# Six columns of zero rows a batch instead of seven, with one shared column for the few rows beyond them

**Chip, cores, metric.** One core of one Trainium2 chip. The time is that of the device for one execution, in microseconds (us).

## The reference

```python
# scores (8, 2048, 2048) f32, values (8, 2048, 2560) f32
best_j = np.argmax(scores, axis=2)
gathered = values[b_idx, best_j, :].copy()
out = np.zeros_like(values)
np.add.at(out, (b_idx, best_j, slice(None)), gathered)
```

An output row is thus the value row with the same number, times how many score rows picked it: about 750 rows of a batch are picked once, 550 more often, and 750 never.

## The kernel before

VectorE counts for every row how often it was picked, and builds lists of row numbers. GpSimd then issues indirect transfers of 128 entries each: copies of once-picked rows straight from `values` to `out`, gathers of the oftener picked (ScalarE scales them, then they are scattered), and scatters of a row of zeros to the rows never picked. An entry that names no row holds a number past the end and is skipped.

```python
ZCAP, MCAP = 7, 5          # zero columns and gather columns of a batch, 128 entries each
ZLAST = 12                 # zero columns of the last batch
FETCH = {2: 5, 3: 12}      # rows of other traffic booked for DMA engines 2 and 3
...
# value_steps(b): after the counts
first = (NT, NT // 2, 4)[min(b, 2)]        # row copies issued ahead of the gathers
for t in range(first):
    copy_once(t)
...
def zeros(columns):
    for k in columns:
        scatter(zrow[:], zi[:, k:k + 1], free_running)
        if rest:
            copy_once(rest.pop(0))
...
nz = ZLAST if b == B - 1 else ZCAP
if b == 0: ...
else:
    gathers()                              # five, with a row copy after each
    zeros(range(ZHEAD))                    # four
for k in range(MCAP):
    scatter(staged[k], mi[:, k:k + 1], ...)
if b > 0:
    zeros(range(ZHEAD, nz))
```

In the last batch a routine on VectorE (`level_engines`) adds up how many rows each of the 16 DMA engines has to move, and deals that batch's zero rows so that the engines come out equal.

## Time and profile before

| | value | how to read it |
|---|---|---|
| time, median of the first three runs | 824.42 us (824.17 to 825.19) | the spread is larger than the effect that is looked for |
| 4-byte packets of the GpSimd queue | 17,974 | skipped entries and completion marks |
| zero-row transfers | 61 | 7 x 7 + 12 |
| rows moved | 20,762 | the work itself, not touched by the change |

The lines of the page and of the stages stand in the prediction.

### The profile page before, as it was taken

The numbers are of one execution on the slowest core, as the hardware profiler recorded it, in microseconds if no ns is written. First come the engines' busy times: TensorE is split into PE (matmuls) and PEld (weight loads), VectorE is DVE, ScalarE is ACT, GpSimd is POOL, SyncE is SP. The second block draws the span as 40 slices with busy tenths as digits, with TensorE's granted clock in tenths as the row PEclk, the third lists the DMA queues.
The fourth block names the chain that finished last, engine by engine and source line by source line (L and its number), as shares of the span: only waits on it lengthen the run. The fifth ranks groups of instructions, "written<-read, shape, count | busy, mean of one in ns | idle before, by whom it ended". The sixth has DMA issues, their size and how long they took to land.

```text
span 824.0 us, 2978 instructions
## 1 busy us (share of the span) xinstructions
PE 31.8 (4%) x786; PEld 29.1 (4%) x786; DVE 600.3 (73%) x737; ACT 168.1 (20%) x107; POOL 271.3 (33%) x277
## 2 busy tenths in 40 slices
PE   0211210000000000000000000000000000000000
PEld 0111110000000000000000000000000000000000
DVE  5887779999999999999999999999998000000000
ACT  6664730041012100023000032000320230230140
POOL 0027241011233504201513200615166356346442
DMA  9999999999999999999999999999999999999997
GB/s 385 426 437 429 433 412 410 441 419 425 427 423 427 428 427 435 429 428 420 429 427 421 429 428 430 433 428 412 426 425 424 423 427 422 424 424 422 425 425 288
DMA packets 44949, 347.12 MB, mean 421 GB/s; under 512 B 18662, under 2 KB 18662, under 8 KB 18662
## 3 DMA queue, kind: packets, MB, share of 16 engines
q0 software_dynamic: 38736, 212.67, 62.1%
q1 hardware_dynamic: 6192, 134.22, 38.0%
q8 instruction: 6, 0.10, 0.0%
q14 instruction: 15, 0.12, 0.0%
HBM read 354.42 MB, written 300.15 MB: 794 GB/s over the span
## 4 chain that ended last, share of the span: by engine, by line
DMA 35%; DVE 27%; another core or an unknown queue 23%; ACT 5%; POOL 5%; issue 4%; PE 0%; SPq 0%; ACTq 0%; POOLq 0%; DVEq 0%
DMA room<-in_values_dram,many_i 23%; DVE am L201 9%; DVE mx L200 9%; DMA out_dram<-room,many_i 8%; DVE mx L224 5%; ACT room L417 4%; DMA room<-in_scores_dram 4%; POOL out_dram L33 3%; ACT less L227 2%; POOL out_dram L182 2%; POOL room L177 1%; DVE oh L378 1%; DVE oh_lo L210 1%; DVE sole L234 0%
## 5 line engine op out<-in xcount | busy, mean ns | idle before, releaser
L201 DVE FIND_INDEX8 am<-mx,room 128x8 uint32<-128x2048 f32 x96 | 219.3, 2285 | 0.0
L200 DVE MAX8 mx<-room 128x8 f32<-128x2048 f32 x96 | 218.7, 2278 | 0.0
L417 ACT ACTIVATE room<-room,many_c 128x2560 f32<-128x2560 f32 x40 | 96.6, 2426 | 587.6 <-DMA room<-in_values_dram,many_i 587.6
L33 POOL DMA_INDIRECT out_dram<-in_values_dram,ones_i x128 | 130.3, 1018 | 106.3 <-DVE m L349 67.9
L182 POOL DMA_INDIRECT out_dram<-room,many_i x40 | 38.7, 966 | 258.0 <-ACT room L417 254.9
L177 POOL DMA_INDIRECT room<-in_values_dram,many_i x40 | 41.2, 1029 | 155.2 <-DMA out_dram<-room,many_i 137.0
L224 DVE MAX8 mx<-room 128x8 f32<-128x2048 f32 x32 | 72.8, 2286 | 11.4 <-DMA room<-in_scores_dram 11.4
L227 ACT ACTIVATE less<-room,mx 128x2048 bf16<-128x2048 f32 x32 | 64.0, 2001 | 38.4 <-DVE sole L234 17.4
L182 POOL DMA_INDIRECT out_dram<-zrow,zero_i x61 | 60.1, 985 | 18.6 <-issue 18.3
L218 PE MATMUL cnt_ps<-oh_hi,oh_lo 128*128 128x16 bf16 x96 | 6.1, 174 | 418.0 <-DVE oh_hi L214 418.0
L218 PEld LDWEIGHTS <-oh_lo 128*128 128x128 bf16 x96 | 6.3, 104 | 417.9 <-DVE oh_lo L210 397.9
L237 PEld LDWEIGHTS <-less 128*128 128x128 bf16 x512 | 16.1, 104 | 83.3 <-ACT less L227 59.6
L378 DVE TENSOR_TENSOR oh<-lo,fill_f 128x2048 f16<-128x2048 uint32 x8 | 18.3, 2291 | 0.3
L237 PE MATMUL cnt_ps<-sole,less 128*128 128x1 bf16 x512 | 18.1, 165 | 0.0
L210 DVE TENSOR_TENSOR oh_lo<-lo,lane_f 128x512 bf16<-128x512 uint32 x24 | 16.6, 693 | 0.4
L234 DVE TENSOR_SCALAR sole<-n_less 128x1 bf16<-128x1 f32 x32 | 4.8, 149 | 14.9 <-ACT less L227 14.7
L201 DVE MATCH_VALUE_LOAD am<-mx,room 128x8 f32 x96 | 8.8, 92 | 3.3
L235 PE MATMUL cnt_ps<-sole,minus 128*128 128x16 bf16 x32 | 5.5, 172 | 82.9 <-DVE sole L234 81.1
L396 PE MATMUL l_ps<-put,oh 128*128 128x32 f16 x128 | 4.7, 188 | 70.9 <-DVE put L393 70.9
L396 PEld LDWEIGHTS <-oh 128*128 128x128 f16 x128 | 4.6, 104 | 72.0 <-DVE oh L378 61.6
L227 ACT ACTIVATION_READ_ACCUMULATOR less<-room,mx 128x1 f32 x32 | 6.0, 186 | 0.0
L206 DVE TENSOR_SCALAR lo<-am 128x4 uint32<-128x4 uint32 x24 | 5.3, 222 | 0.8
(104 smaller groups left out, 80.7 us busy)
## 6 DMA issues: line engine op xcount, KB each, us to landing
room<-in_scores_dram SPq DMA_DIRECT2D x24, 4096.0 KB, 17.5
room<-in_scores_dram SPq DMA_DIRECT2D x9, 2048.0 KB, 13.1
room<-in_scores_dram SPq DMA_DIRECT2D x8, 1024.0 KB, 5.8
room<-in_scores_dram SPq DMA_DIRECT2D x2, 3072.0 KB, 13.9
out_dram<-in_values_dram,ones_i POOLq DMA_INDIRECT x128
out_dram<-zrow,zero_i POOLq DMA_INDIRECT x61
room<-in_values_dram,many_i POOLq DMA_INDIRECT x40, 45.0
out_dram<-room,many_i POOLq DMA_INDIRECT x40, 46.5
```

What stands on the lines that cost most here:

```text
L33: return eng.add_instruction(ins)
L177: note(nc.gpsimd.indirect_dma_start(out=v, out_offset=None, in_=values_flat[:, :], in_offset=bass.IndirectOffsetOnAxis(ap=idx, axis=0), bo ...
L182: note(nc.gpsimd.indirect_dma_start(out=out_flat[:, :], out_offset=bass.IndirectOffsetOnAxis(ap=idx, axis=0), in_=v, in_offset=None, bound ...
L200: nc.vector.max(out=mx[:], in_=rows)
L201: nc.vector.max_index(out=am[:, g, :], in_max=mx[:], in_values=rows)
L210: nc.vector.tensor_tensor(out=oh_lo[:], in0=lo[:].unsqueeze(2).to_broadcast([P, G, P]), in1=lane_f[:].unsqueeze(1).to_broadcast([P, G, P]) ...
L218: nc.tensor.matmul(out=cnt_ps[:], lhsT=oh_lo[:, k, :], rhs=oh_hi[:, k, :], start=(t == G - 1 and k == 0), stop=(t == NT - 1 and k == G - 1))
L224: nc.vector.max(out=mx[:], in_=rows)
L227: nc.scalar.activation(out=less[:], in_=rows, func=mybir.ActivationFunctionType.Sign, bias=mx[:, 0:1], scale=-1.0, accum_out=n_less[:])
L237: nc.tensor.matmul(out=cnt_ps[:, c:c + 1], lhsT=less[:, c * P:(c + 1) * P], rhs=w, start=False, stop=(t == NT - 1 and c == NT - 1))
L378: nc.vector.tensor_tensor(out=oh[:], in0=lo[:].unsqueeze(2).to_broadcast([P, NT, P]), in1=fill_f[:].unsqueeze(1).to_broadcast([P, NT, P]), ...
L417: nc.scalar.activation(out=v, in_=v, func=mybir.ActivationFunctionType.Copy, bias=0.0, scale=mc[:, k:k + 1])
```

## The change

Its intent: batches 0 to 6 have 748 to 780 rows of zeros. Six columns hold 768, so the seventh is nearly empty. It is dropped, and the rows beyond 768 of all seven batches go to one column at the very end. VectorE has to work out each such row's place in it.

```diff
-    ZCAP, MCAP = 7, 5
+    ZCAP, MCAP = 6, 5
+    left_n, left_f, unfit: three small tiles, filled at the start        (abridged)
 # level_engines
+        nc.vector.tensor_scalar(out=left_e[:], in0=up_f[:], scalar1=left_n[:, 0:1], scalar2=None, op0=ALU.add)
+        (two more: the shared column's rows join the engines' loads)
-        first = (NT, NT // 2, 4)[min(b, 2)]
+        first = (NT, NT // 2, 5)[min(b, 2)]
 # value_steps, b < B - 1, after the ranks
+            nc.vector.tensor_scalar(out=n_b[:], in0=tots[:, 0, b:b + 1], scalar1=-float(ZCAP * P), scalar2=0.0, op0=ALU.add, op1=ALU.max)
+            (ten more: does the batch's rest fit, move its ranks behind those of earlier batches)
 # value_steps, after the lists
+            (three more: take the batch's entries over into left_f)
 # value_steps, at its end
         if b > 0:
             zeros(range(ZHEAD, nz))
+        if b == B - 1:
+            scatter(zrow[:], left_i[:, 0:1], free_running)
```

More of the change, by code (lines that the diff above doesn't have):

```diff
@@ L118 @@
     tots = consts.tile([P, 2, B], FP32)
+    left_n = consts.tile([P, 1], FP32)
+    nc.vector.memset(left_n[:], 0.0)
+    left_f = consts.tile([P, 1], FP32)
+    nc.vector.memset(left_f[:], BIG)
+    unfit = consts.tile([P, 1], FP32)
+    nc.vector.memset(unfit[:], 0.0)
     most = consts.tile([P, 1], FP32)
@@ L151 @@
     ones_i = ctx.enter_context(nc.sbuf_tensor([P, B * NT], INT32))
+    left_i = ctx.enter_context(nc.sbuf_tensor([P, 1], INT32))
     zero_i = ctx.enter_context(nc.sbuf_tensor([P, B * NT], INT32))
@@ L281, in level_engines @@
         nc.vector.tensor_reduce(out=load[:, 1, :], in_=share[:, :, B:2 * B], op=ALU.add, axis=X)
+        left_e = lev.tile([P, NE], INT32)
+        nc.vector.tensor_scalar(out=left_e[:], in0=up_f[:], scalar1=left_n[:, 0:1], scalar2=None, op0=ALU.add)
+        nc.vector.tensor_single_scalar(out=left_e[:], in_=left_e[:], scalar=4, op=ALU.logical_shift_right)
+        nc.vector.tensor_tensor(out=load[:, 0, :], in0=load[:, 0, :], in1=left_e[:], op=ALU.add)
         work = lev.tile([P, NE], FP32)
@@ L368, in value_steps @@
             nc.vector.tensor_scalar(out=rank[:, c, :], in0=base[:, c, :], scalar1=off_ps[:, c:c + 1], scalar2=None, op0=ALU.add)
+        unfit_b = fin.tile([P, 1], FP32)
         if b == B - 1:
             level_engines(rank[:, 0, :])
+        else:
+            n_b = fin.tile([P, 1], FP32)
+            nc.vector.tensor_scalar(out=n_b[:], in0=tots[:, 0, b:b + 1], scalar1=-float(ZCAP * P), scalar2=0.0, op0=ALU.add, op1=ALU.max)
+            fit_b = fin.tile([P, 1], FP32)
+            nc.vector.tensor_tensor(out=fit_b[:], in0=n_b[:], in1=left_n[:], op=ALU.add)
+            nc.vector.tensor_scalar(out=unfit_b[:], in0=fit_b[:], scalar1=float(P), scalar2=BIG, op0=ALU.is_gt, op1=ALU.mult)
+            nc.vector.tensor_tensor(out=unfit[:], in0=unfit[:], in1=unfit_b[:], op=ALU.max)
+            nc.vector.tensor_single_scalar(out=fit_b[:], in_=fit_b[:], scalar=float(P), op=ALU.is_le)
+            shift_b = fin.tile([P, 1], FP32)
+            nc.vector.tensor_tensor(out=shift_b[:], in0=left_n[:], in1=fit_b[:], op=ALU.mult)
+            past = fin.tile([P, NT], FP32)
+            nc.vector.tensor_scalar(out=past[:], in0=rank[:, 0, :], scalar1=float(ZCAP * P), scalar2=shift_b[:, 0:1], op0=ALU.is_ge, op1=ALU.mult)
+            nc.vector.tensor_tensor(out=rank[:, 0, :], in0=rank[:, 0, :], in1=past[:], op=ALU.add)
+            nc.vector.tensor_tensor(out=n_b[:], in0=n_b[:], in1=fit_b[:], op=ALU.mult)
+            nc.vector.tensor_tensor(out=left_n[:], in0=left_n[:], in1=n_b[:], op=ALU.add)
+            nc.vector.tensor_tensor(out=tots[:, 0, b:b + 1], in0=tots[:, 0, b:b + 1], in1=n_b[:], op=ALU.subtract)
         hi = fin.tile([P, 2, NT], U32)
@@ L409, in value_steps @@
         nc.vector.tensor_copy(mc, l_ps[:, NM:2 * NM])
+        if b < B - 1:
+            x = 2 * NM + ZCAP
+            left_b = fin.tile([P, 1], FP32)
+            nc.vector.scalar_tensor_tensor(out=left_b[:], in0=e[:, x:x + 1], scalar=float(b * S - 1), in1=l_ps[:, x:x + 1],
+                                           op0=ALU.add, op1=ALU.add)
+            nc.vector.tensor_tensor(out=left_b[:], in0=left_b[:], in1=unfit_b[:], op=ALU.add)
+            nc.vector.tensor_tensor(out=left_f[:], in0=left_f[:], in1=left_b[:], op=ALU.min)
+        else:
+            nc.vector.tensor_copy(left_i[:], left_f[:])
         rest = list(range(first, NT))
@@ L472 @@
             pass
-        full = fin.tile([1, 2], FP32)
-        nc.vector.tensor_reduce(out=full[:, 0:1], in_=tots[0:1, 0, 0:B - 1], op=ALU.max, axis=mybir.AxisListType.X)
-        nc.vector.tensor_reduce(out=full[:, 1:2], in_=tots[0:1, 1, :], op=ALU.max, axis=mybir.AxisListType.X)
+        full = fin.tile([1, 1], FP32)
+        nc.vector.tensor_reduce(out=full[:], in_=tots[0:1, 1, :], op=ALU.max, axis=mybir.AxisListType.X)
         worst = fin.tile([P, 1], BF16)
@@ L481 @@
         nc.vector.tensor_single_scalar(out=over[:, 3:4], in_=sole_ps[0:1, :], scalar=-float(P), op=ALU.is_gt)
-        nc.vector.tensor_single_scalar(out=over[:, 0:1], in_=full[:, 0:1], scalar=float(ZCAP * P), op=ALU.is_gt)
-        nc.vector.tensor_single_scalar(out=over[:, 1:2], in_=full[:, 1:2], scalar=float(MCAP * P), op=ALU.is_gt)
+        nc.vector.tensor_single_scalar(out=over[:, 0:1], in_=unfit[0:1, :], scalar=0.0, op=ALU.is_gt)
+        nc.vector.tensor_single_scalar(out=over[:, 1:2], in_=full[:], scalar=float(MCAP * P), op=ALU.is_gt)
         nc.vector.tensor_single_scalar(out=over[:, 2:3], in_=most[0:1, :], scalar=float(ZLAST * LE), op=ALU.is_gt)
```

## The prediction

> **What bounds the kernel now.** I began with the page: busy shares, the 40 slices, the DMA queues. VectorE looks like the fullest engine (73%), but the slices say when.
>
> ```profile
> DVE  5887779999999999999999999999998000000000
> ...
> DMA  9999999999999999999999999999999999999997
> GB/s 385 426 437 429 433 412 410 441 419 425 427 423 427 428 427 435 429 428 420 429 427 421 429 428 430 433 428 412 426 425 424 423 427 422 424 424 422 425 425 288
> ...
> q0 software_dynamic: 38736, 212.67, 62.1%
> q1 hardware_dynamic: 6192, 134.22, 38.0%
> ```
>
> VectorE is full until slice 31 (640 us) and then has nothing to do; the DMA engines are full from the first slice to the last. The two queues' packet times add up to 100.1% of 16 engines' span. The same in stages, with each engine's busy time, clock, DMA share and GB/s at the end of a line:
>
> ```profile
> 550.00:640.00 90.00, 2.74 (x52) 2.40 (x52) 86.27 (x137) 12.03 (x5) 42.31 (x42) 1.00 1.01 423
> 640.00:720.00 80.00, 0.00 (x0) 0.00 (x0) 0.07 (x1) 16.87 (x7) 37.27 (x38) 1.00 1.02 425
> 760.00:800.00 40.00, 0.00 (x0) 0.00 (x0) 0.00 (x0) 12.14 (x5) 17.56 (x18) 1.00 1.02 424
> 800.00:824.00 24.00, 0.00 (x0) 0.00 (x0) 0.00 (x0) 0.00 (x0) 7.74 (x8) 1.00 0.75 306
> ```
>
> The rate is the same while VectorE works (423) and when it has finished (425), and the DMA share is 1.01 to 1.02 throughout. So the kernel ends when its DMA engines have moved their packets. The chain of waits names VectorE and GpSimd for parts of the span, but in none of them did the DMA engines run dry. From the packet records in the trace I counted, moment by moment, how many packets were in flight: between the first load and the last 15 us, missing engines add up to 0.11 us of the span; in the last 8 us, in which engines finish one after another, to 3.6 us. At the start it is the 2.8 us before the first load.
>
> So the question is what one packet costs. The records sort by size. There are 20,762 packets of 10,240 B (a row of values or of output), 386 ns each on average, 501.4 us of the span when divided over 16 engines; the score loads are 313.2 us. Then queue 0 has 17,974 packets of 4 B, recorded at 9 ns each, 10.1 us over 16 engines. Of those, 269 indirect transfers x 16 = 4,304 are completion marks. The 269 transfers have 269 x 128 = 34,432 index entries; less the 20,762 rows that leaves 13,670: the entries whose index is out of range. A skipped entry thus still costs a 4-byte packet, but a tiny one.
>
> **What the Trainium skill says.** "DMA: Bandwidth & Descriptors", section "Issuing engines are not separate DMA queues": transfers of all engines run on the same 16 DMA engines and interleave. The trace agrees: 62.1% + 38.0% fill one span. The same page, note to "Measured (HBM→SBUF, 128 partitions, SWDGE, issued from GpSimd)": the smallest transfer is about 10.5 ns for each of 64 packets. The trace has 9 ns for a 4-byte packet, and less when they follow each other (below). "Perfetto Trace Analysis", section "DMA Instruction — SWDGE (GPSIMD)": the profiler's end for such an instruction is the end of descriptor generation, not of the movement. The trace agrees: a gather takes GpSimd 1.03 us and lands after 45.0 us (median). So a removed column's GpSimd time is not a transfer's time. No page says what an out-of-range index costs.
>
> **What is removed.** Each batch but the last issues seven columns of 128 zero rows. The seed is fixed, so I counted: rows that no score picks are 761, 777, 780, 771, 778, 770, 748 in batches 0 to 6, and 746 in batch 7. Six columns hold 768. So the seventh held 0, 9, 12, 3, 10, 2, 0 rows: 36 in all, beside 860 skipped entries. The change drops seven columns and adds one, in which the 36 fit (limit 128, so the slow path for overflow isn't taken).
>
> No row is dropped: 36 move to the end. What goes is 6 x 128 = 768 skipped entries and 6 x 16 = 96 marks. Per DMA engine that is 6 x (8 + 1) = 54 packets of 4 B. For their cost I have two readings. The recorded duration is 9 ns. But in the closing run of the trace, where one engine has only such packets left (46 of them), they start 5.9 ns apart; and fitting 16 engines' time in 5-us pieces of 590 to 805 us to the rows and 4-byte packets in them gives 382 ns a row and 5.7 +- 0.9 ns a 4-byte packet. So 54 x 5.9 = 0.32 us to 54 x 9 = 0.49 us; I take 0.4 us.
>
> The GpSimd time that goes is more, and beside the path:
>
> ```profile
> L182 POOL DMA_INDIRECT out_dram<-zrow,zero_i x61 | 60.1, 985 | 18.6 <-issue 18.3
> ```
>
> 985 ns and 0.30 us of issue: 6 x 1.28 = 7.7 us, of an engine busy 33%.
>
> **What is added.** For each batch but the last, 11 small VectorE instructions after the counts and 3 after the lists; for the last 4; at the start 3 fills; one reduction less at the end: 104 more. Existing chains of this kind start one every 0.19 to 0.21 us (the levelling of the last batch, 128x16 and 128x1). So 14 x 0.2 = 2.8 us a batch, 7 x 2.8 = 19.6 us, and about 1 us for the rest: VectorE should end near 660 us instead of 639.92. That is beside the path: the batch 7 index lists are ready at 639.0 and their first gather is issued here, so some 86 us of 107 remain.
>
> ```profile
> 745.00 0.97 POOL L33 DMA_INDIRECT out_dram<-in_values_dram,ones_i  x1 [0.30 <-issue]
> 746.27 1.04 POOL L177 DMA_INDIRECT room<-in_values_dram,many_i  x1 [0.30 <-issue]
> ```
>
> **What moves.** One row copy per later batch goes from behind the removed column to before the gathers. After the last batch's scatters GpSimd had 8 zero columns and 3 copies; now 8 zero columns, 2 copies and the shared column, also 11 transfers. Its last issue stays near 810, some 14 us ahead of the DMA's end.
>
> **The spread over engines.** The last batch's zeros are dealt so that engines get equal rows. I did this arithmetic from the inputs. Most engines come to 1,301 rows by the kernel's reckoning, before and after alike (before: engine 9 1,288, 12 1,283, 15 1,295; after: 1,288, 1,285, 1,293). The engine that ends last can be told by its closing packets: rows and gaps match the once-picked rows of partitions 32 to 39 (engine 4) in the last two copies of batch 7. It has 1,301 rows in both; so the imbalance of 3.6 us isn't repaired, nor should it grow. Sum: 824.42 - 0.4 = 824.0.
>
> **Rivals.**
> 1. Skipped entries cost what GpSimd spends on them. Then 7.7 us go: 816.7, just under 1%. Against: GpSimd is idle two thirds of the time and the DMA share never falls while it works.
> 2. VectorE's extra time starves the DMA. For: in the first half GpSimd once or twice catches up with VectorE.
>
> ```profile
> 282.31 1.40 POOL L177 DMA_INDIRECT room<-in_values_dram,many_i  x1 [0.31 <-DVE hi L208]
> ```
>
> By then VectorE would be some 8 us late (3 x 2.8). But counting rows issued less rows landed, 1,190 were queued at that moment: 1,190 x 0.386 / 16 = 28.7 us even with no score loads beside them. The lowest stock between 80 and 800 us that I trust is 361 rows at 220 us (8.7 us), where GpSimd waits for a buffer and not for VectorE. (In batch 7 this count is rough, as its columns are filled unevenly.) I give it 1 to 3 us and a chance of a few in a hundred: 825 to 827.
> 3. The shared column is issued last, so it delays the end by its own 1.27 us: 825.7. Against: 14 us of rows are still queued then, and its 36 rows, two or three an engine, are counted in the levelling.
> 4. The last engine changes by a row or two, or an extra instruction fetch (8 KB, 309 ns in the records) falls to it: +-0.8 us.
>
> **Range and chances.** The step of 0.4 us is smaller than the spread of three runs before (824.17 to 825.19). Around 824.0 I put rival 4's 0.8 below, and 1.0 above for it with the spread of the runs: 823.2 to 825.0. A 2% step is 16.5 us; even rival 1 makes less than half of that. Within 2%: 0.98.
>
> **What would show it.** Queue 0's packets should fall by 864 to 37,872, with 212.67 MB unchanged; zero-row transfers from 61 to 55 with the shared one counted; VectorE's last instruction near 660 us and its busy time up by some 15 us; the DMA share still 1.01 to 1.02 in every stage up to 800 us, and the fall at the end as long as before. I am wrong if a stage before 800 us shows a share under 1.00 (VectorE or a buffer wait starves the DMA), if the closing fall gets longer or shorter by over a microsecond (the levelling moved), or if the time falls by several microseconds with the bytes unchanged (a skipped entry costs more than its packet).

## The result, and the profile after

Five runs each: 823.57 us median (822.98 to 824.11) against 824.47 (824.17 to 825.19). The ratio is 0.9987 with a 95% interval from 0.9973 to 1.0002. A ratio here is the mean time of one kernel's fast runs over that of the other's of the same rounds, so not quite the ratio of the medians. The predicted 824.0 lies 0.43 us from the measured median, inside the range; the step was 0.90 us where 0.4 was forecast, though the interval covers both.

The changed kernel's page: the VectorE slices, queue 0, and the zero-row group (the shared column is a group of its own, one transfer).

```profile
DVE  5889899999999999999999999999999200000000
...
q0 software_dynamic: 37872, 212.67, 62.1%
...
L190 POOL DMA_INDIRECT out_dram<-zrow,zero_i x54 | 53.8, 995 | 16.5 <-issue 16.5
```

864 packets fewer with the same megabytes, and 54 + 1 transfers: as forecast. The stages of the changed kernel that answer to those of before:

```profile
550.00:640.00 90.00, 1.99 (x35) 1.79 (x35) 86.99 (x143) 12.03 (x5) 40.22 (x41) 1.00 1.01 423
640.00:720.00 80.00, 0.75 (x17) 0.61 (x17) 3.50 (x18) 16.88 (x7) 36.21 (x36) 1.00 1.02 424
760.00:800.00 40.00, 0.00 (x0) 0.00 (x0) 0.00 (x0) 12.03 (x5) 16.58 (x18) 1.00 1.02 425
800.00:824.00 24.00, 0.00 (x0) 0.00 (x0) 0.00 (x0) 0.00 (x0) 6.73 (x7) 1.00 0.72 292
```

In these stages share and rate are as before until 800 us; the last window looks emptier mostly because this execution's span is 822.3 us and not 824.0. And the end of GpSimd's timeline:

```profile
806.55 0.97 POOL L190 DMA_INDIRECT out_dram<-zrow,zero_i  x1 [0.31 <-issue]
807.82 0.97 POOL L190 DMA_INDIRECT out_dram<-zrow,left_i  x1 [0.30 <-issue]
```

The shared column is issued at 807.82, well ahead of the end of the DMA, as the last issue was before (809.08).

**Where the time went, by packets.** The recorded packet times of one execution of each kernel, divided over 16 engines:

| us | before | after | difference |
|---|---|---|---|
| rows of 10,240 B | 501.43 | 500.77 | -0.66 |
| 4-byte packets of queue 0 | 10.15 | 9.63 | -0.52 |
| score loads | 313.16 | 313.13 | -0.03 |
| missing engines in the last 15 us | 3.57 | 3.37 | -0.19 |

The second line is the intended gain as the records count it (9 ns each; at the 5.9 ns of their spacing it is 0.3 us). The first line was not forecast: the same rows took less time. In the kernel before, rows are not all 385 ns; 1.85 us of the 501.43 is stretch beyond that, against 1.19 us after. By time, 0.95 us of the stretch before lies between 122 and 132 us, against 0.04 us after. The stages of the two kernels there, before first:

```profile
120.00:124.00 4.00, 0.00 (x0) 0.00 (x0) 3.96 (x3) 0.00 (x0) 3.09 (x4) 1.00 1.06 404
124.00:130.00 6.00, 0.00 (x0) 0.00 (x0) 5.96 (x5) 0.00 (x0) 3.10 (x4) 1.00 1.02 367
```

```profile
120.00:124.00 4.00, 0.00 (x0) 0.00 (x0) 4.00 (x3) 0.00 (x0) 0.00 (x0) 1.00 1.05 425
124.00:130.00 6.00, 0.00 (x0) 0.00 (x0) 5.93 (x6) 0.00 (x0) 0.00 (x0) 1.00 1.00 413
```

The reader should set the last two columns side by side: a DMA share of 1.02 with 367 GB/s. The engines count as busy, and yet they move less. The prediction took a full share for a full rate and so passed over this dip. The Trainium skill warns of it: "Perfetto Trace Analysis", section "Identifying the Most-Contended Engine", says that with 16 DMA engines occupancy misleads, and to go by HBM utilization.

What goes with these 6 us: counting rows in order of issue, the kernel before serves rows 438 to 748 of queue 0 from 120.5 to 130.5 us. Rows up to 748 are batch 0's copies of once-picked rows, from HBM to HBM, and between 121.0 and 128.4 us no score load moves beside them. After row 748 the zero rows begin and the rate is back above 400. In the changed kernel the same copies are spread over 120.5 to 138 us with score loads between them.

That copies without loads are slow as such is not so, however. By the same count of issue the kernel before also moves nothing but copies from 691 to 696 us, after its last score load, and each of these 204 rows took 385 ns:

```profile
691.00:696.00 5.00, 0.00 (x0) 0.00 (x0) 0.00 (x0) 0.00 (x0) 3.90 (x4) 1.00 1.01 418
```

So the missing loads are found beside the dip, and what slows the rows stays open.

Why the loads are missing: VectorE ends batch 1 at 111.5 us in the kernel before and at 103.1 us after, for all its added work; score loads follow it, as they need its buffers. ScalarE makes the difference. Its timeline in batch 1, kernel before:

```profile
70.30 2.00 ACT L227 ACTIVATE less<-room,mx 128x2048 bf16<-128x2048 f32 x1 [0.16 <-DVE mx L224]
...
77.69 2.00 ACT L227 ACTIVATE less<-room,mx 128x2048 bf16<-128x2048 f32 x1 [5.30 <-remote]
...
85.52 2.00 ACT L227 ACTIVATE less<-room,mx 128x2048 bf16<-128x2048 f32 x1 [5.73 <-issue]
```

and the changed kernel:

```profile
72.31 2.00 ACT L235 ACTIVATE less<-room,mx 128x2048 bf16<-128x2048 f32 x1 [0.16 <-DVE mx L232]
...
74.71 2.00 ACT L235 ACTIVATE less<-room,mx 128x2048 bf16<-128x2048 f32 x1 [0.30 <-DVE sole L242]
...
76.91 2.00 ACT L235 ACTIVATE less<-room,mx 128x2048 bf16<-128x2048 f32 x1
```

Two instructions start over 5 us after their predecessor ended, and the profile's view names no engine that held them ("remote", "issue"). VectorE in turn waits for ScalarE, which is the dip to 7 in its slices (`5887779` before, `5889899` after). All kernels tried are of one of these two kinds, called late and early from here.

The semaphore events in the traces (a semaphore is the counter by which one engine signals another) lead one step further back, to TensorE. ScalarE's two waits end when a semaphore rises that TensorE's matmuls of L237 raise, which free the `less` buffer: at 77.62 and 85.44 us in the kernel before, 6.6 and 12.2 us after the ends that the profile gives those matmuls (70.98 and 73.23; such ends are modelled). (The n-th rise of the semaphore was set beside the n-th matmul that raises it; up to 63 us the two agree within 0.1 us in every trace.) From 63 to 86 us all nine late traces have this delay, growing to between 9.8 and 12.4 us; the five early traces have none above 0.1 us. Why TensorE signals late there is open. It is no instruction that differs: the kernel before and b_z10 (below) execute the same ones on every engine until past 77 us, and one is late and the other early.

The chip was not held fixed, either. The four traces of the first call, all early, are from chip 14; the eight of the later calls, all late, are from chips 13, 7 and 0. The chip of the first trace before (late) and after (early) is not on record. No kernel was traced twice on chips known to differ, so the kind may belong to the chip and not to the build. If so, the kernel before, run beside the others on the same chip, was of their kind too, and the kind explains nothing of the ratios. No run here decides it.

### The profile page after: what moved, and what is told of

Read it like the earlier page. It is cut to its first block, busy times and chain, and to the rows that moved or that the text cites. A ratio compares the mean times of both kernels' runs of the same rounds, so it can differ in the third digit from the quotient of the medians.

```text
span 822.3 us, 3076 instructions
## 1 busy us (share of the span) xinstructions
PE 31.8 (4%) x786; PEld 29.1 (4%) x786; DVE 613.6 (75%) x841; ACT 168.0 (20%) x107; POOL 265.5 (32%) x271
## 3 DMA queue, kind: packets, MB, share of 16 engines
q0 software_dynamic: 37872, 212.67, 62.1%
HBM read 354.42 MB, written 292.29 MB: 786 GB/s over the span
## 4 chain that ended last, share of the span: by engine, by line
another core or an unknown queue 44%; DMA 39%; ACT 7%; DVE 6%; issue 1%; POOL 1%; SPq 0%; ACTq 0%; PE 0%; POOLq 0%; DVEq 0%
DMA room<-in_values_dram,many_i 18%; DMA out_dram<-room,many_i 17%; DVE mx L232 5%; ACT room L456 5%; DMA room<-in_scores_dram 4%; ACT less L235 2%; POOL out_dram L190 1%; DVE oh L408 0%; SPq L254 0%; DVE sole L242 0%; ACTq L456 0%; PE cnt_ps L245 0%; DVE ez L413 0%; DVE put L423 0%
## 5 line engine op out<-in xcount | busy, mean ns | idle before, releaser
L33 POOL DMA_INDIRECT out_dram<-in_values_dram,ones_i x128 | 130.5, 1019 | 106.6 <-DVE m L361 68.2
L190 POOL DMA_INDIRECT out_dram<-zrow,zero_i x54 | 53.8, 995 | 16.5 <-issue 16.5
```

The lines of the kernel that those rows point to most:

```text
L33: return eng.add_instruction(ins)
L190: note(nc.gpsimd.indirect_dma_start(out=out_flat[:, :], out_offset=bass.IndirectOffsetOnAxis(ap=idx, axis=0), in_=v, in_offset=None, bound ...
```

## The experiments

The theory at first: the packets are the gain. Rivals: something else of the change (VectorE's work, tile layout, order of the copies), later: the kind. Each table entry is five runs (six of a_lev4b) against the kernel before on the same chip, and one trace. "Packets" are 4-byte packets for each DMA engine, against the kernel before; "stretch" is what rows took beyond 385 ns, over 16 engines; "closing" is what the missing engines of the last 15 us add up to.

| run | chip | packets | kind | median us | ratio (95%) | stretch us | closing us |
|---|---|---|---|---|---|---|---|
| before (first trace) | - | 0 | late | 824.47 | 1 | 1.85 | 3.57 |
| after (first trace) | - | -54 | early | 823.57 | 0.9987 (0.9973 to 1.0002) | 1.19 | 3.37 |
| a_again | 14 | -54 | early | 823.77 | 0.9987 (0.9973 to 1.0001) | 1.49 | 1.83 |
| a_empty | 14 | +9 | early | 823.75 | 0.9990 (0.9976 to 1.0003) | 1.48 | 2.19 |
| b_z10 | 14 | +189 | early | 825.49 | 1.0009 (0.9995 to 1.0023) | 1.59 | 2.56 |
| b_z16 | 14 | +567 | early | 836.46 | 1.0148 (1.0134 to 1.0162) | 5.36 | 5.08 |
| b_again | 13 | 0 | late | 825.33 | 1.0005 (0.9992 to 1.0019) | 1.85 | 3.58 |
| b_first5 | 13 | 0 | late | 824.78 | 1.0000 (0.9987 to 1.0014) | 2.14 | 1.61 |
| a_cap7 | 13 | +9 | late | 824.95 | 1.0001 (0.9987 to 1.0014) | 1.57 | 2.49 |
| a_lev4 | 13 | -54 | late | 824.05 | 0.9994 (0.9980 to 1.0008) | 1.76 | 1.60 |
| a_memset | 7 | -54 | late | 824.23 | 0.9995 (0.9982 to 1.0008) | 1.96 | 1.25 |
| b_memset | 7 | 0 | late | 824.66 | 0.9994 (0.9981 to 1.0007) | 1.70 | 2.40 |
| a_lev4b | 7 | -54 | late | 823.62 | 0.9989 (0.9977 to 1.0001) | 2.32 | 2.54 |
| b_memset3 | 0 | 0 | late | 825.17 | 0.9995 (0.9981 to 1.0008) | 2.10 | 3.41 |

The kernel before, run beside the others, drifted from call to call, that is from chip to chip (824.59, 824.82, 824.98, 825.46 median), so ratios are compared and not times.

### First call: is it the packets?

**a_again.** The changed kernel unaltered.

> The changed kernel once more, unaltered, to see how far its 0.90 us of gain (824.47 to 823.57, ratio 0.9987, interval 0.9973 to 1.0002) is the change and how far it is the spread of the runs. Theory (a removed skipped entry saves 5.9 to 9 ns on its DMA engine, 54 a DMA engine): 0.3 to 0.5 us under the kernel before. Rival (the change saves something else as well, for instance by an earlier start of batch 1 on VectorE): 0.9 us again.

Ratio 0.9987 again. Over both calls the mean of ten runs is 823.55 us against 824.64 of the fourteen runs of before beside them. The gain of 1 us thus came twice, though each ratio's interval just reaches 1, and it is twice what the packets were to give.

**b_z10, b_z16.** The kernel before with more columns in which every entry is skipped.

```diff
-    ZCAP, MCAP = 7, 5
+    ZCAP, MCAP = 10, 5        (b_z16: 16, 5)
```

> The kernel before with ten zero columns a batch instead of seven, so 21 more columns in which every entry is skipped; result unchanged. Theory: 21 x 9 = 189 more 4-byte packets on each DMA engine, at 5.9 to 9 ns 1.1 to 1.7 us longer than the kernel before. Rival 1 (a column costs what GpSimd spends on it): 21 x 1.28 = 27 us. Third way: the packets fit into gaps between rows: under 0.3 us.

> The kernel before with sixteen zero columns a batch instead of seven, 63 more columns with nothing but skipped entries; result unchanged. Theory: 63 x 9 = 567 more 4-byte packets on each DMA engine, 3.3 to 5.1 us longer, three times the step of ten columns, unless GpSimd, which then spends 11.5 us more on each batch, lets the queue run dry (DMA share under 1.00 before 800 us). Rival 1: 81 us. Third way (gaps): under 1 us.

b_z10: 0.9 us by the medians (0.7 us by the ratio) for 21 columns, a little under the forecast of 1.1 to 1.7. Rival 1 of the prediction (27 us) is out. b_z10's page has the 21 columns:

```profile
DVE  5889899999999999999999999999994000000000
...
L182 POOL DMA_INDIRECT out_dram<-zrow,zero_i x82 | 81.3, 991 | 25.0 <-issue 25.0
```

The first line shows that it is of the early kind. If the kernel before was late beside it, b_z10 looks cheaper than it is. Against the changed kernel, which is early too, it is 0.0022 of the time, 1.8 us, for 243 packets a DMA engine: 7.5 ns each, between the recorded 9 ns and the spacing of 5.9 ns.

b_z16 costs 11.9 us, more than 567 packets do (3.3 to 5.1 us forecast). Its stages (b_z16) show why:

```profile
690.00:700.00 10.00, 0.00 (x0) 0.00 (x0) 0.00 (x0) 0.00 (x0) 7.56 (x9) 1.00 1.00 358
700.00:756.00 56.00, 0.00 (x0) 0.00 (x0) 0.00 (x0) 12.03 (x5) 33.18 (x35) 1.00 1.02 420
756.00:766.00 10.00, 0.00 (x0) 0.00 (x0) 0.00 (x0) 0.00 (x0) 7.80 (x8) 1.00 0.97 346
```

In the two 10-us stretches just after GpSimd has issued empty columns one after another (nine in a row from 744.43 us on, before the second), the rate falls to 358 and 346 and the share once to 0.97. An empty column takes GpSimd 1.27 us and gives each DMA engine 9 packets of 5.9 ns, 0.05 us of work, so the stock of rows shrinks. It is not used up: missing engines add up to 0.3 and 0.4 us there, while rows took 421 and 427 ns on average instead of 385. Over the whole trace, 9.8 us longer than that of before, the rows took 3.5 us more and missing engines 2.8 us; what remains, 3.5 us, is 6 ns for each of the 567 packets. The expectation had named a dry queue as the exception; it is one part, and slow rows are another. Either way the "GpSimd is beside the path" argument has a limit: true for one spare column a batch, no more for ten.

**a_empty.** The seventh column put back as one that is always empty, the rest of the change kept.

```diff
             zeros(range(ZHEAD, nz))
+            if b < B - 1:
+                scatter(zrow[:], zi[:, NT - 1:NT], free_running)     # (and the same in batch 0)
```

> The changed kernel with the removed seventh column put back as one that is always empty (index column 15), in seven batches; everything else of the change stays: VectorE's added work, the shared column, the levelling. Theory: 7 x 9 = 63 packets a DMA engine come back, so 0.4 to 0.6 us longer than the changed kernel, and 0.05 us above the kernel before. Rival (the gain came from the other parts of the change): it stays at the time of the changed kernel.

Mean 823.80 against a_again's 823.50: 0.3 us longer, where 0.4 to 0.6 was expected, but 0.8 us faster than the kernel before, which has 9 packets fewer. Taken at their means, the packets are a part of the gain at most, and the theory in its simple form fell; the interval (0.9976 to 1.0003) still holds the 1.0001 that the theory asked for.

### Second call: which other part?

**b_again.** The kernel before unaltered, as a control.

> The kernel before, unaltered, as a control: ratio 1.000, within 0.15% either way. It also gives a second trace of that kernel. In the first one DMA engine 4 ended 3.8 us after the mean of the 16 engines; in the changed kernel's two traces it ended 2.0 and 2.1 us after it, with the same 1,301 rows. If that is the spread of one run, the second trace shows 2 to 3 us; if it belongs to the kernel, 3.5 us or more again.

Ratio 1.0005. Its second trace repeats the first in detail: 1.85 us of stretch, 3.58 us of closing, DMA engine 4 again 3.8 us after the mean of the 16 engines. So one run's chance is not needed to explain them; but the changed kernel's two traces differ (1.19 and 1.49 us of stretch, 3.37 and 1.83 of closing), so a build does not fix them either.

(The ends of single engines were had by following back the chain of packets of each engine: order and pattern of real and skipped entries are known from the inputs, and a row takes 381 ns to the next packet, a small one 5.9 ns. For the kernel before, the last 305 packets matched on 13 of 16 engines, and on the others more than 110.)

**a_cap7.** The changed kernel with seven columns, so that nothing is left over: VectorE's added work and an empty shared column remain.

```diff
-    ZCAP, MCAP = 6, 5
+    ZCAP, MCAP = 7, 5
-        first = (NT, NT // 2, 5)[min(b, 2)]
+        first = (NT, NT // 2, 4)[min(b, 2)]
```

> The changed kernel with seven columns a batch again, so that nothing is left over: the index lists and the levelling are those of the kernel before, row copies in the old order; what remains of the change is VectorE's added work, three small tiles and one always empty shared column at the end (9 packets a DMA engine). Theory (only packets count): the kernel before + 0.05 to 0.1 us, 824.6 to 824.7. Rival (the 0.8 us that stayed in a_empty come from VectorE's added work or the tile layout): 823.8.

Ratio 1.0001, as the theory said: VectorE's added work, the tiles and the extra transfer neither cost nor gain anything that can be measured (the interval is 1.1 us either way). Rival 2 of the prediction (VectorE starves the DMA, 1 to 3 us) is out in nearly all of its range.

**b_first5.** The order of the row copies alone.

```diff
-        first = (NT, NT // 2, 4)[min(b, 2)]
+        first = (NT, NT // 2, 5)[min(b, 2)]
```

> The kernel before with the one row copy per batch moved ahead of the gathers (five instead of four), as in the change, and nothing else. Theory: the same packets, the time of the kernel before within 0.3 us. Rival (the order of the copies gave the 0.8 us): 823.8.

Ratio 1.0000: the order gives nothing that can be measured.

**a_lev4.** An attempt at a better version: the levelling books 7 rows more for engine 4.

```diff
-    FETCH = {2: 5, 3: 12}
+    FETCH = {2: 5, 3: 12, 4: 7}
```

> The changed kernel with 7 rows of other traffic booked for DMA engine 4 in the levelling, since it ended 2.0 to 2.3 us after the mean in three traces of the changed kernel and its variant: its zeros of the last batch fall from 38 to about 32, the others rise by half a row. If the end is set by that engine: its end comes 2.3 us earlier, the others 0.2 us later, and the next engine in line, 1.5 to 2 us after the mean, sets the end: 0.3 to 1 us under the changed kernel. If the last engine is a different one each time: within 0.3 us of it.

Engine 4 now ended 0.6 us before the mean, as booked, but engine 10 ended 1.8 us after it. The ratio is 0.9994, worse than that of the changed kernel. Its VectorE ends batch 1 at 111.7 us: it is of the late kind, as thought because of its one more small fill at the start. This, and that a_cap7, b_first5 and b_again were late as well and the four of the first call early, led to the theory of the kinds.

### Third call: do the kinds matter?

**a_memset.** The changed kernel with one fill that does nothing.

```diff
-    FETCH = {2: 5, 3: 12}
+    FETCH = {2: 5, 3: 12, 4: 0}
```

> The changed kernel with one more small fill by VectorE at the start, which writes a zero over a zero; packets and levelling are those of the changed kernel. Theory: the traces so far come in two kinds. In one, ScalarE starts two instructions of batch 1 some 3 us late each (72 to 88 us), VectorE ends that batch at 111.5 instead of 103 us, and at 124 to 130 us the rows take 450 to 600 ns instead of 385, which costs 0.4 to 0.7 us; the kernel before, its twin, the one with the moved copies, a_cap7 and a_lev4 are of this kind, the changed kernel, its twin, a_empty and the ones with 10 and 16 columns are of the other. If this kernel falls into the late kind, as a_lev4 with the same fill did: 823.9 to 824.3, 0.3 to 0.5 us slower than the changed kernel and 0.3 to 0.5 us faster than the kernel before (its 54 packets). If it stays in the early kind: 823.5 to 823.7 as the changed kernel. Rival (the late rows at 124 us do not matter for the end): 823.6 also with late rows.

It fell into the late kind, and its time into the range forecast for it: 824.23 us, ratio 0.9995. With nothing added but a zero written over a zero, some 0.7 us of 1.1 are gone (0.9995 against 0.9987). But it ran on chip 7 and a_again on chip 14, and each ratio lies in the other's interval, so neither the fill nor the kind is shown to have cost it. The dip is back too; a_memset's stage:

```profile
124.00:130.00 6.00, 0.00 (x0) 0.00 (x0) 5.93 (x6) 0.00 (x0) 2.68 (x3) 1.00 1.02 391
```

**b_memset** (the same fill in the kernel before) and, in a fourth call, **b_memset3** (three of them).

```diff
-    FETCH = {2: 5, 3: 12}
+    FETCH = {2: 5, 3: 12, 4: 0}              (b_memset3: 4: 0, 5: 0, 6: 0)
```

> The kernel before with the same extra fill of a zero over a zero. If that shakes it into the early kind (VectorE ends batch 1 near 101 to 103 us, no slow rows at 124 us): 0.4 to 0.6 us under the kernel before, and 0.3 to 0.5 us above the changed kernel, which are its 54 packets. If it stays in the late kind: the time of the kernel before within 0.2 us. Rival (the two kinds do not matter): the time of the kernel before in either kind.

> The kernel before with three extra fills of a zero over a zero at VectorE's start, as many as the change adds; the fourth corner is missing so far, the packets of before in the early kind. If it falls into the early kind (VectorE ends batch 1 near 101 to 103 us, no slow rows at 124 us): by the early kinds' slope (b_z10 over the changed kernel, 1.9 us for 243 packets a DMA engine, 7.7 ns each) 0.4 us above the changed kernel's 823.5, so 823.9 to 824.2, ratio 0.9992 to 0.9995. If it stays in the late kind: ratio 0.9995 to 1.0005. Rival (the kind does not matter, the change's other parts do): ratio 1.000 in the early kind too.

Both stayed late (VectorE ends batch 1 at 111.5 and 111.7 us), with ratios of 0.9994 and 0.9995, so b_memset moved further than the 0.2 us expected of it. Two builds with fills that do nothing stand 0.4 to 0.5 us under the kernel before, and the unaltered b_again 0.4 us above it: a spread as wide as what the packets were forecast to give. The corner that would have closed the square, the packets of before in the early kind, was not reached.

**a_lev4b.** a_lev4 with two fills made one.

```diff
-    left_n = consts.tile([P, 1], FP32)
-    nc.vector.memset(left_n[:], 0.0)
+    counts = consts.tile([P, 2], FP32)
+    nc.vector.memset(counts[:], 0.0)
+    left_n, unfit = counts[:, 0:1], counts[:, 1:2]
-    unfit = consts.tile([P, 1], FP32)
-    nc.vector.memset(unfit[:], 0.0)
```

> a_lev4 (7 rows booked for DMA engine 4) with two of the start's fills made one, so that it has as many as the changed kernel. In the early kind it should have the changed kernel's mean end of the 16 DMA engines and a last engine 1.5 us instead of 2 to 3.5 us after it: 822.5 to 823.2, the fastest of all. In the late kind 0.4 us more.

Late all the same, so the number of fills alone does not decide the kind. 823.62 us median of six runs, 823.49 to 826.45; ratio 0.9989 with an interval up to 1.0001. It isn't shown to beat the changed kernel.

## Why the prediction was right or wrong

- **Right: the bound.** The kernel stays bound by its DMA engines and within 2%. Packets (37,872), megabytes (212.67), transfers (55) and the end of GpSimd's issue (807.82 + 0.97 us) came as worked out.
- **Right: what is beside the path.** GpSimd's saved time is worth nothing near 7.7 us: 21 columns more, 27 us of GpSimd, cost 0.9 us. VectorE's work neither: a_cap7 has it and stands at 1.0001.
- **Right in size, but only within the noise: the packets.** 54 packets at 5.9 to 9 ns were to give 0.3 to 0.5 us. Early kernels alone, from -54 over +9 to +189 packets, have ratios of 0.9987, 0.9990 and 1.0009, or 7.5 ns a packet from end to end: 54 x 7.5 = 0.4 us. Late kernels alone: a_memset at 0.9995 against a mean of 0.9999 for the five late kernels with the old packets (1, 1.0005, 1.0000, 0.9994, 0.9995): 0.3 us. Each single ratio has an interval of some 0.0013 either way, 1.1 us, so none of these differences is proved by itself, and the late traces do not bear theirs out: the mean end of the 16 DMA engines is 818.3 us in the three with 54 packets fewer (a_memset, a_lev4, a_lev4b) and 818.3 in the five with the old packets.
- **Wrong: the sum left out a term.** The step reads "Sum: 824.42 - 0.4 = 824.0", and measured was a step of 0.9 to 1.1. In the first pair of traces the largest term that the sum lacks is the rows' own duration, which the prediction took as 386 ns before and after: it measured 0.66 us less. The ground for leaving it out was that "in none of them did the DMA engines run dry", read from the number of packets in flight. They did not run dry; in the kernel before they were slow for 6 us, and in the traced execution of the changed one they were not. That this term made the rest of the gain is argued and not shown. Between like packets, early is 0.0008 below late (0.9987 against a_memset's 0.9995), some 0.7 us; the difference in stretch in the traces is 0.5 to 0.8 us (1.19 and 1.49 against 1.96). The two agree, but rest on one late build of the changed kernel, on another chip, and the closing of the traces (3.37, 1.83 and 1.25 us) scatters as much.
- **Wrong: VectorE's end.** "VectorE should end near 660 us", and it ended at 644.5. Two parts: batch 1 ended 8.4 us earlier than before, which is the kind; and a batch's 14 instructions took some 2.2 us instead of 2.8. In a_memset, late like the kernel before, VectorE ends at 651.8, 11.7 us after the 640.1 of before; among the early ones, 644.5 is 15.5 us after b_z10's 629.0. About 20 were forecast. The spacing of 0.2 us was taken from a chain in which each instruction needs the one before; some of the added ones don't, and then start 0.08 us apart. Nothing hung on it.
- **Half right: the last engine.** "The engine that ends last" was DMA engine 4, and the imbalance was to stay. In the first trace after the change engine 10 ends last, 3.6 us after the mean, and engine 4 2.1 us; in the second it is engine 4 again, at 2.0. The closing of 3.6 us became 3.4 and 1.8.

What stays open: why TensorE signals late from 63 to 86 us in some traces (neither the number of fills nor of columns decides it, and it may be the chip), what slows the rows at 124 us, and how the gain of about 1 us divides between packets, kind and chance. No kernel with the old number of packets was traced in the early kind, and no kernel in both kinds; one build traced on several chips would tell whether the kind is the chip's.

## What to carry to other kernels

A skipped entry of an indirect transfer costs the DMA engines almost nothing, so dropping 860 of them is worth half a microsecond at most; look for such gains only after the rate, not just the share, has been read stage by stage. When an effect is smaller than a tenth of a per cent, make a build with an edit that does nothing and see how far that moves the time: here such builds and an unaltered one lay as far apart as the forecast effect, so such a version is accepted for its packets, not for its time. And trace the kernel before on the same chip as each variant: where all variants of one call differ from all of another, the chip is a rival to every explanation by the build.

## What the Trainium skill lacked or had wrong

- "DMA: Bandwidth & Descriptors": it doesn't say what an out-of-range index of an indirect transfer costs. Here it is a 4-byte packet, recorded at 9 ns, 5.9 ns apart in a run of them, and about 7.5 ns by the time of whole kernels.
- The same page gives how the 128 partitions of an SBUF tile are dealt to the engines, but not how the 128 rows of a copy from HBM to HBM are. In the traces engine k took entries 8k to 8k + 7 of each copy (305 closing packets matched in pattern on 13 of 16 engines).
- "HBM Reference", section "Specifications (TRN2)", gives about 716 GB/s for an HBM domain, and says that a core streaming alone reaches about 425 GB/s. No page says what this means for copies from HBM to HBM, which read and write it. Here copies alone moved 346 and 361 GB/s from 124 to 128 us in the two traces of before, but 418 and 422 GB/s from 691 to 696 us. As an estimate, with each byte counted as read and as written, the latter is some 840 GB/s, above that page's 716; whether both tensors lie in one domain no run shows. So that figure does not explain the slow rows at 124 us.
- No page that I read says how the HBM bytes of the profile are counted. They include rows that were skipped: 300.15 MB are given as written before and 292.29 MB after, a difference of 768 rows of 10,240 B, though both kernels write the same output.
